# Head stages, residual loads and one more seven-product pair in an encoder layer on one core

## The chip, the cores and the metric

The kernel runs on one core of one Trainium2 chip. The metric is the device time of one execution in microseconds (us). Three executions of the kernel before the change took 1923.64, 1925.68 and 1930.04 us; the median is 1925.68.

The core's engines each work through their own list of instructions in order: TensorE (PE: products and transposes; PEld is its loading of weights), VectorE (DVE), ScalarE (ACT), GpSimd (POOL) and SyncE (SP, which here only issues DMA transfers). They wait for each other through semaphores. An instruction that waits holds up everything behind it on its engine or queue.

## The reference

One encoder layer over 256 tokens with 4096 features, float32.

```python
h = rms_norm(x, g_mix)
proj = h @ w_in            # c_q | c_kv | k_rope | gate_a | q_b | k_b | v_b | gate_b
# A: latent attention, 16 heads of 128 (+64 rotary)
q_a = rms_norm(c_q, g_q_latent) @ w_uq
kv = rms_norm(c_kv, g_kv_latent) @ w_ukv
y_a = rms_norm(mla_attention(q_a, kv, k_rope), g_out_mla) * silu(gate_a)
# B: dilated attention, 16 heads of 128, three (window, dilation) patterns
y_b = rms_norm(dilated_mixture_attention(q_b, k_b, v_b), g_out_dil) * silu(gate_b)
x = x + concat(y_a, y_b) @ w_out
ple = p @ w_ple
gate = sigmoid(rms_norm(x, g_ple) @ w_ple_gate)
out = rms_norm(x + ple * gate, g_final)
```

## The kernel before

**Products.** Every float32 operand is split into a high and a low half (ScalarE writes the high half, VectorE subtracts it from the source and writes the low half, `split`). A product of a 128-row piece is three matmuls: high by high, high by low, low by high (`mm`). Weights come from memory in tiles of 128 x 1024 (512 KB, the tile `raw`, four buffers, `RAW` at line 1738) through SyncE's queue, are split, and are used at once for two token tiles and two column halves: four products, twelve matmuls 512 wide.

**Seven-product pairs.** Two such row tiles can be taken together as a two-by-two block product with seven products in place of eight (Strassen's scheme in Winograd's form). `fast_steps` (line 1167) makes the four steps of a pair: more sums on VectorE, one product less on TensorE. The sums of the activations are made ahead (`x_sums`, `y_sums`). `FAST_QKV` (line 1552) says how many pairs each of the six blocks of q, k and v takes out of its 32 row tiles, in the order q, k, v of the first half and then of the second; `LEAD_QKV` how many plain steps come first; `spread` (line 1502) mixes plain steps and the steps of the pairs.

**The planner.** The order of instructions on all engines is written by the program itself while it builds. The main loop runs the product steps one after another. Between products it calls `advance` (line 417), which resumes side tasks: generators such as a head's attention. `Clock` (line 67) keeps an estimated time for each engine and each tile. A task has a due time, `due[task]`; it is resumed when that is at most `SOON` = 0.3 us past the estimated time of TensorE, `clock.free["pe"]`. `resume` (line 404) sets the due time from what the task has issued and, if the task yields a number, from that number.

**A head** (`attend`, line 573) has three stages that begin on TensorE. Dilated heads first transpose q and k. Then come the scores, into PSUM bank `s` (reserved by `take`, line 368); the softmax on VectorE and ScalarE; the transposes of the probabilities, into bank `t0` or `t1` (reserved by `turned`, line 378, which other tasks also use for their transposes: gates, normalised residuals, latents); a split; and the values, into bank `o`, reserved by `take`. The 16 dilated heads run beside the latent projection (some 509 to 682 us in the profile), the 16 latent heads beside their own up-projections and the first w_out products (some 1049 to 1224 us). The flag `"x dead"` (line 1621) is set between the two, after the gates' projections.

**After the latent heads**: `y_stats` and `gate_rest` normalise and gate the head outputs (transposes again), `split_y` splits them into `yT`, `y_sums` makes the sums for the pairs in tile T1. w_out is made as two half chunks (columns of residual blocks 6 and 7, the rows that need only the dilated heads), then three wide blocks of 1024 columns (`WIDE_O`) with 6, 6 and 4 pairs, then the other halves of blocks 6 and 7. The pairs of the first wide block use tile B4 for their differences, which held one of the gates.

**Residual x.** `load_res(c)` (line 1026) loads the 512 columns of x that residual block c adds, 512 KB, into tile T0 to T7. Before, all eight go through GpSimd's queue. Blocks 6 and 7 are asked for with the half chunks; blocks 2k and 2k + 1 at steps 8 and 9 after the start of wide block k (line 1657), once all latent heads are recorded. They are added when the block's pairs are done (`out_mid`).

All instructions that the planner records carry line 176 of its helper in the profile; groups are told apart by their tiles. Tile names there: `m`, `s`, `o`, `t` are PSUM banks, `raw` weights as loaded, `hi` and `lo` the halves, `Ah`, `Al`, `B`, `T`, `Q` the large tiles that are reused, weight halves among them.

Of the kernel before, what the change touches and what calls it, by code (L numbers as in the profile page):

```python
# [18 lines left out]
P = 128  # L19
# [3 lines left out]
HEADS = 16  # L23
# [186 lines left out]
def encoder_layer(ctx: ExitStack, tc: tile.TileContext, x, p, positions, g_mix, w_in, g_q_latent, w_uq,  # L210
                  g_kv_latent, w_ukv, g_out_mla, g_out_dil, w_out, w_ple, g_ple, w_ple_gate, g_final,
                  c_inv, c_dist, out):
    whole, clock = tc.nc, Clock()
    nc = Engines(whole, clock)
    x, p, out = x[0], p[0, 0], out[0]
# [10 lines left out]
    def slot(tag, shape, dtype=F32):  # L226
        names[tag] = names.get(tag, 0) + 1
        return clock.made(sp.tile([P, *shape], dtype, tag=tag, name=f"{tag}_{names[tag]}"), tag)
# [58 lines left out]
    G, at = {"mix": gT[:, :32]}, 0  # L287
# [11 lines left out]
    def turn_gains(i, at, n):  # L299
        tag = yield from turned()  # L300
        tp = bank(tag, [2 * S])
        nc.tensor.transpose(tp[:, :n], gains[:n, i], ident[:n, :n])
        yield
        nc.scalar.activation(gT[:, at:at + n], tp[:, :n], AF.Copy)
        give(tag)
# [51 lines left out]
    class Flags(set):  # L357
        at = {}
# [5 lines left out]
    flags, urgent, waiting, running = Flags(), [], [], []  # L364

    locks = set()

    def take(*tags):

        while any(t in locks for t in tags):  # L370
            yield
        locks.update(tags)
        yield max(clock.ready(t) for t in tags)

    def give(*tags):
        locks.difference_update(tags)
# [1 line left out]
    def turned():  # L378

        while True:  # L380
            open_ = [t for t in turns if t not in locks]
            if open_:
                tag = min(open_, key=clock.ready)
                locks.add(tag)
                yield clock.ready(tag)
                return tag
            yield

# [5 lines left out]
    begun, due = [-20.0], {}  # L394
# [3 lines left out]
    def spawn(task, later=False):  # L398
        urgent.append(task)
        due[task] = 0.0  # L400
        if later:
            lazy.add(task)

    def resume(pool, task):
        while True:
            clock.stage = 0.0
            got = next(task, "end")
            due[task] = max(clock.stage, due.get(task, 0.0), got if isinstance(got, float) else 0.0)
            if got == "end":
                pool.remove(task)  # L410
                due.pop(task, None)
                lazy.discard(task)
                return
            if not isinstance(got, float) or due[task] > clock.free["pe"] + SOON:
                return
# [76 lines left out]
    def done_a(i):  # L492
        def task(ps):
# [63 lines left out]
            pe = slot("T7", [2, S], F32R)  # L557
            T7["pe"] = pe
            tag = yield from turned()
            tp = bank(tag, [2, S])  # L560
            for t in range(NT):
# [11 lines left out]
    def attend(h, q_src, k_src, pe, v, y, dil):  # L573
# [19 lines left out]
        else:  # L593
            qT, kT = q_src, k_src
        at_s, at_o = "s", "o"
        yield from take(at_s)
        s = bank(at_s, [NT, S])
        for t in range(NT):
# [419 lines left out]
    x1 = {}  # L1018
# [5 lines left out]
        return tuple(q[:, kt % 4] for q in yT[kt // 4])  # L1024

    def load_res(c):
        before = {6: ("pe", 1), 7: ("scored", 0, HEADS - 1)}.get(c)
        while not (before in flags if before else all(("head", 0, h) in flags for h in range(HEADS))):
            yield
        x1[c] = slot(f"T{c}", [NT, 512])  # L1030
        nc.gpsimd.dma_start(x1[c], x[:, 512 * c:512 * (c + 1)].rearrange("(t p) k -> p t k", p=P))
        flags.add(("res", c))

    X1_TAGS = "Ah3", "Al3", ("B7a", "B7b"), "B4", "B6", "Al1", "B2", "B3"
# [220 lines left out]
    def out_mid(k, blk):  # L1255
        def task():
            ps, u = blk.ps, slot("Q0", [Q])
            x11, x21, x12, x22 = (x1[2 * k + h][:, t] for h in range(2) for t in range(NT))

            def add(d, a, b):  # L1260
                nc.vector.tensor_tensor(d, a, b, op=ALU.add)

            nc.scalar.activation(u, ps["M1"], AF.Copy)
            add(x11, x11, ps["M1"])
            add(u, u, ps["M6"])
            add(x12, x12, ps["M5"])
            add(x12, x12, u)
            yield
            add(u, u, ps["M7"])
            add(x22, x22, ps["M5"])  # L1270
            add(x21, x21, u)
            add(x22, x22, u)
            yield
        return task

    def out_done(k, blk):
        def task():
            quarters = ((0, 0, "M2"), (1, 1, "X"), (0, 1, "M3"), (1, 0, "M4"))
            for t, h, m in quarters:
                xc = x1[2 * k + h][:, t]  # L1280
                nc.vector.tensor_tensor(xc, xc, blk.ps[m], op=ALU.add)
            yield
            turns_ = [x1_turn(2 * k + h) for h in range(2)]
            for h in range(2):
                for t in range(NT):
                    c = 2 * k + h
                    nc.scalar.activation(junk, x1[c][:, t], AF.Square, accum_out=ss1[:, t, c:c + 1])
                yield from turns_[h]
        return task
# [198 lines left out]
    steps = []  # L1488
# [13 lines left out]
    def spread(n, lead, trail, extra=()):  # L1502

        rest = 32 - 2 * n - lead - trail
        order, debt, k = ["c"] * lead, 0.0, 0
        rate = (n * sum(FAST_COST) + rest * PLAIN_COST) / (n * sum(FAST_TIME) + rest * PLAIN_TIME)
        while k < 4 * n or rest:
            if k < 4 * n and (debt <= 0 or not rest):
                order.append("f")
                debt += FAST_COST[k % 4] - rate * FAST_TIME[k % 4]  # L1510
                k += 1
            else:
                order.append("c")
                rest -= 1
                debt += PLAIN_COST - rate * PLAIN_TIME
        order += ["c"] * trail
        for at in extra:
            order.insert(at, "e")
        return order

    def lay(blk, order, mid, done, ple=None):
        last = max(i for i, o in enumerate(order) if o == "f")
        n = order.count("f") // 4
        fast = (x for j in range(n) for x in blk.fast_steps(j))
        rest = list(range(2 * n, 16)) + list(range(16, 32))
        if blk.late:
            rest = rest[16 - 2 * n:] + rest[:16 - 2 * n]
        plain_ = (x for kt in rest for x in blk.plain_step(kt))
        for i, kind in enumerate(order):
            new = {"f": lambda: [next(fast)], "c": lambda: [next(plain_)], "e": lambda: ple}[kind]()  # L1530
            if i == last:
                new[-1].after = mid
            if i == len(order) - 1:
                new[-1].after = done
            for x in new:
                x.ring, x.ring_id = blk.ring, blk
            steps.extend(new)
        return len(steps) - len(order) + last

    def hook(at, f):  # L1540
        hooks.setdefault(at, []).append(f)

    def only(*tags):
        def go():
            turns[:] = tags
        return go
# [2 lines left out]
    G_BANKS = "m2", "m3", "s", "o", "m0", "m1", "t0", "t1"  # L1549
    H_BANKS = "m0", "m1", "t0", "t1", "m2", "m3", "s", "o"  # L1550
    Y_BANKS = "s", "o", "t0", "t1", "m0", "m1", "m2", "m3"
    FAST_QKV, LEAD_QKV = (3, 7, 7, 8, 8, 6), (18, 4, 4, 4, 4, 8)
    FAST_G, LEAD_G = (4, 7, 7, 7), (14, 6, 6, 4)
    FAST_O, LEAD_O = (6, 6, 4), (4, 5, 4)

# [24 lines left out]
    def allow(blk, tag, when):  # L1580
        allowed[tag, blk] = when
# [71 lines left out]
    for k in range(WIDE_O):  # L1653
        if k:
            hook(len(steps), only(*(("s", "o"), ("t0", "t1"))[k - 1]))
        for h in range(2):
            hook(len(steps) + 8 + h, lambda c=2 * k + h: spawn(load_res(c)))
        order = spread(FAST_O[k], LEAD_O[k], 4)
        blk = Block(w_out[:, 1024 * k:1024 * (k + 1)], lhs_y, y_s, "y_sums", order, lambda kt: [("yT", kt // 4)],
                    (G_BANKS, H_BANKS)[k % 2], "B4" if k < 2 else "Al1",  # L1660
                    WP + (["Ah3", "Al3", ("B7a", "B7b")], [("B7a", "B7b")], ["B3"])[k])
        blk.row = lambda kt: (kt + 16) % 32
        if k == 0:
            blk.fast_needs = [("gated", 0, c) for c in range(4)]
            blk.holds = blk.fast_needs
        else:
            blk.turn_needs = [("x1T", 2 * k - 2), ("x1T", 2 * k - 1)]
        lay(blk, order, out_mid(k, blk), out_done(k, blk))
        end = len(steps) - 1
        if k == 0:  # L1670
            for tag in ("Ah3", "Al3"):
                allow(blk, tag, lambda i, end=end: ("yT", 7) in flags and i < end)
            allow(blk, ("B7a", "B7b"), lambda i: ("gated", 0, 1) in flags)
        elif k == 1:
            allow(blk, ("B7a", "B7b"), lambda i, end=end: i < end)
# [119 lines left out]
    steps = [Old(i, *x) if isinstance(x, tuple) else x for i, x in enumerate(steps)]  # L1795
# [152 lines left out]
```

## Time and profile before

| what | us |
| --- | --- |
| median of three executions | 1925.68 |
| lowest, highest | 1923.64, 1930.04 |
| the profiled execution, its own time | 1922.69 |
| span of its instructions | 1920.9 |
| TensorE busy | 1897.0 |
| VectorE busy | 1635.0 |
| ScalarE busy | 1115.9 |

The profile is of one execution. A span of a matmul reaches beyond the start of the next one, since matmuls are pipelined: the time from start to start is what a matmul costs TensorE, and a short pause may not show as idle time at all. PEld, the loading of weights, shows such pauses better. A row of the waits names who waited for whom, the total in us, how often, and the longest. A row of the time line gives start, duration, what ran, and in square brackets the idle time before it and what ended it. A row of the chain of waits gives start and duration of one piece of the chain that ended last. A row of the stretches gives, for each engine, the busy time in it, then the granted TensorE clock, the busy share of the 16 DMA engines and GB/s.

### The profile page before, as it was taken

The numbers are of one execution on the slowest core, as the hardware profiler recorded it, in microseconds if no ns is written. First come the engines' busy times: TensorE is split into PE (matmuls) and PEld (weight loads), VectorE is DVE, ScalarE is ACT, GpSimd is POOL, SyncE is SP. The second block draws the span as 40 slices with busy tenths as digits, with TensorE's granted clock in tenths as the row PEclk, the third lists the DMA queues.
The fourth block names the chain that finished last, engine by engine and source line by source line (L and its number), as shares of the span: only waits on it lengthen the run. The fifth ranks groups of instructions, "written<-read, shape, count | busy, mean of one in ns | idle before, by whom it ended". The sixth has DMA issues, their size and how long they took to land.

```text
span 1920.9 us, 25936 instructions
## 1 busy us (share of the span) xinstructions
PE 1897.0 (99%) x9454; PEld 1615.9 (84%) x9454; DVE 1635.0 (85%) x2270; ACT 1115.9 (58%) x1518; POOL 40.8 (2%) x56
## 2 busy tenths in 40 slices
PE   9999999999999999999999999999999999999997
PEld 7888888888899988888888998878888887888887
DVE  6999989898877789899998678888887989889865
ACT  7655656564577755556556555656555555656543
POOL 1000000000000100000000001100000000000000
PEclk9999999999999999999999999999999999999999
DMA  8566766666654566666667444576666556566665
GB/s 274 185 204 215 219 207 201 198 206 197 181 154 136 148 194 192 194 207 195 213 203 199 131 121 143 160 257 202 196 195 199 182 195 215 190 220 204 214 196 176
DMA packets 159024, 370.61 MB, mean 193 GB/s; under 512 B 28548, under 2 KB 70640, under 8 KB 158640
## 3 DMA queue, kind: packets, MB, share of 16 engines
q1 hardware_dynamic: 157008, 361.82, 60.6%
q0 software_dynamic: 1888, 7.14, 1.1%
q8 instruction: 74, 1.21, 0.3%
q14 instruction: 54, 0.44, 0.1%
HBM read 364.72 MB, written 4.19 MB: 192 GB/s over the span
## 4 chain that ended last, share of the span: by engine, by line
PE 90%; DVE 5%; DMA 2%; ACT 1%; issue 1%; SPq 0%; DVEq 0%; ACTq 0%
PE m L176 51%; PE t L176 17%; PE s L176 11%; PE o L176 11%; DVE lo L176 1%; DVE T L176 1%; DMA raw<-in_w_out_dram 1%; DVE B L176 1%; DVE Al L176 1%; ACT hi L176 1%; ACT T L176 0%; DVE st L176 0%; DMA raw<-in_w_in_dram 0%; DMA raw<-in_w_ple_gate_dram 0%; DVE Ah L176 0%
## 5 line engine op out<-in xcount | busy, mean ns | idle before, releaser
L176 ACT ACTIVATE hi<-raw 128x1024 fp32r<-128x1024 f32 (+3 forms) x453 | 438.1, 976 | 344.5 <-PE t L176 90.0
L176 DVE TENSOR_TENSOR lo<-raw,hi 128x1024 fp32r<-128x1024 f32 (+3 forms) x453 | 502.3, 1118 | 112.5 <-ACT hi L176 109.4
L176 PE MATMUL m<-hi,Ah 128*128 128x512 f32 (+2 forms) x840 | 310.0, 381 | 3.5 <-DVE B L176 2.1
L176 PE MATMUL m<-hi,Al 128*128 128x512 f32 (+3 forms) x832 | 298.6, 372 | 0.0
L176 PE MATMUL m<-lo,Ah 128*128 128x512 f32 (+3 forms) x722 | 269.3, 373 | 0.8 <-DVE lo L176 0.8
L176 PE MATMUL m<-hi,B 128*128 128x512 f32 (+1 forms) x654 | 206.1, 365 | 1.0 <-DVE B L176 1.0
L176 DVE TENSOR_TENSOR B<-raw,B 128x1024 fp32r<-128x1024 f32 (+2 forms) x200 | 184.5, 932 | 16.3 <-ACT B L176 14.7
L176 PEld LDWEIGHTS m<-hi,Ah 128*128 128x128 f32 x840 | 157.9, 188 | 27.2 <-DVE B L176 2.8
L176 PEld LDWEIGHTS m<-hi,Al 128*128 128x128 f32 x832 | 155.9, 188 | 22.4
L176 ACT ACTIVATE B<-raw 128x1024 fp32r<-128x1024 f32 (+1 forms) x126 | 117.6, 941 | 85.1 <-DMA raw<-in_w_in_dram 24.4
L176 PEld LDWEIGHTS m<-lo,Ah 128*128 128x128 f32 x722 | 135.8, 188 | 20.9 <-DVE lo L176 3.1
L176 PEld LDWEIGHTS m<-hi,B 128*128 128x128 f32 x654 | 120.0, 189 | 19.6 <-issue 1.4
L176 PE MATMUL m<-lo,B 128*128 128x512 f32 (+1 forms) x327 | 118.9, 364 | 0.2 <-DVE lo L176 0.2
L176 PE MATMUL m<-B,Ah 128*128 128x512 f32 (+1 forms) x389 | 100.7, 360 | 0.0
L176 DVE TENSOR_TENSOR T<-raw,T 128x512 f32<-128x512 f32 (+2 forms) x101 | 77.8, 778 | 3.1 <-ACT T L176 1.7
L176 PE MATMUL t<-hi,Ah 128*128 128x512 f32 (+1 forms) x209 | 77.4, 386 | 0.0
L176 PEld LDWEIGHTS m<-B,Ah 128*128 128x128 f32 x389 | 66.6, 189 | 11.1 <-DVE B7b L176 0.2
L176 PE MATMUL m<-B,Al 128*128 128x512 f32 (+1 forms) x286 | 75.8, 345 | 0.0
L176 PEld LDWEIGHTS m<-lo,B 128*128 128x128 f32 x327 | 61.8, 189 | 10.2 <-DVE lo L176 1.6
L176 ACT ACTIVATE hi<-B 128x1024 fp32r<-128x1024 f32 x51 | 53.7, 1057 | 22.3 <-issue 8.6
L176 PE MATMUL t<-lo,Ah 128*128 128x512 f32 (+1 forms) x171 | 66.1, 387 | 0.0
L176 DVE TENSOR_TENSOR T<-t,T 128x512 fp32r<-128x512 f32 (+2 forms) x57 | 38.8, 684 | 30.2 <-ACT T L176 30.1
(501 smaller groups left out, 4025.7 us busy)
## 6 DMA issues: line engine op xcount, KB each, us to landing
raw<-in_w_in_dram SPq DMA_DIRECT2D x320, 512.0 KB, 4.3
raw<-in_w_out_dram SPq DMA_DIRECT2D x128, 512.0 KB, 4.5
raw<-in_w_ple_gate_dram SPq DMA_DIRECT2D x128, 512.0 KB, 4.6
raw<-in_w_in_dram SPq DMA_DIRECT2D x48, 384.0 KB, 3.3
raw_q<-in_w_uq_dram SPq DMA_DIRECT2D x32, 256.0 KB, 4.0
raw_k<-in_w_ukv_dram SPq DMA_DIRECT2D x16, 512.0 KB, 4.2
raw<-in_w_in_dram SPq DMA_DIRECT2D x16, 448.0 KB, 3.5
raw_r<-in_w_uq_dram SPq DMA_DIRECT2D x16, 256.0 KB, 3.7
```

Of the source, the lines that this page charges most:

```text
L176: return do(out, *rest, **named)
```

## The change

Three edits:

- A stage that begins on TensorE is handed out later. `take` for bank `s` or `o`, and `turned`, now yield a `Late` number, and `resume` adds 0.3 us to the due time for it, 0.45 us once `"x dead"` is set. This holds for every user of `turned`, heads or not.
- Residual blocks 0 to 5 are loaded through SyncE's queue, the one of the weights; 6 and 7 stay on GpSimd's. Within a wide block the two loads are asked for at steps 6 and 14 in place of 8 and 9, and block 1 waits for the last y sum.
- The third block of q, k and v (v of the first half) takes eight pairs in place of seven.

```diff
+    class Late(float):
+        pass
+
     def take(*tags):
 
         while any(t in locks for t in tags):
             yield
         locks.update(tags)
-        yield max(clock.ready(t) for t in tags)
+        at = max(clock.ready(t) for t in tags)
+        yield Late(at) if tags[0] in ("s", "o") else at
...
                 tag = min(open_, key=clock.ready)
                 locks.add(tag)
-                yield clock.ready(tag)
+                yield Late(clock.ready(tag))
                 return tag
...
             due[task] = max(clock.stage, due.get(task, 0.0), got if isinstance(got, float) else 0.0)
+            if isinstance(got, Late):
+                due[task] += 0.45 if "x dead" in flags else 0.3
...
     def load_res(c):
-        before = {6: ("pe", 1), 7: ("scored", 0, HEADS - 1)}.get(c)
+        before = {1: ("y_sums", 5), 6: ("pe", 1), 7: ("scored", 0, HEADS - 1)}.get(c)
         while not (before in flags if before else all(("head", 0, h) in flags for h in range(HEADS))):
             yield
         x1[c] = slot(f"T{c}", [NT, 512])
-        nc.gpsimd.dma_start(x1[c], x[:, 512 * c:512 * (c + 1)].rearrange("(t p) k -> p t k", p=P))
+        queue = nc.gpsimd if c > 5 else nc.sync
+        queue.dma_start(x1[c], x[:, 512 * c:512 * (c + 1)].rearrange("(t p) k -> p t k", p=P))
...
-    FAST_QKV, LEAD_QKV = (3, 7, 7, 8, 8, 6), (18, 4, 4, 4, 4, 8)
+    FAST_QKV, LEAD_QKV = (3, 7, 8, 8, 8, 6), (18, 4, 4, 4, 4, 8)
...
-            hook(len(steps) + 8 + h, lambda c=2 * k + h: spawn(load_res(c)))
+            hook(len(steps) + 6 + 8 * h, lambda c=2 * k + h: spawn(load_res(c)))
```

## The prediction

> **What bounds the kernel now.** I read the page first, then the busy time by stretches, then the waits of the weight loads, then the time line and the chain of waits where TensorE stood still.
>
> ```profile
> span 1920.9 us, 25936 instructions
> ...
> PE 1897.0 (99%) x9454; PEld 1615.9 (84%) x9454; DVE 1635.0 (85%) x2270; ACT 1115.9 (58%) x1518; POOL 40.8 (2%) x56
> ...
> PEclk9999999999999999999999999999999999999999
> ...
> PE 90%; DVE 5%; DMA 2%; ACT 1%; issue 1%; SPq 0%; DVEq 0%; ACTq 0%
> ```
>
> TensorE is busy 1897.0 of 1920.9 us, at its full clock in every slice, and it is 90% of the chain. So there are two ways to gain: fewer products, or fewer of the pauses in the remaining 23.9 us and in the smaller ones that overlapped spans hide. The stretches say where pauses are:
>
> ```profile
> core 0: us, PE busy (x) PEld busy (x) DVE busy (x) ACT busy (x) POOL busy (x), PEclk, DMA share, GB/s
> 97.00:180.00 83.00, 82.96 (x366) 68.21 (x365) 80.87 (x108) 46.49 (x55) 0.00 (x0) 1.00 0.66 210
> 180.00:262.00 82.00, 82.00 (x363) 67.72 (x363) 75.36 (x86) 48.05 (x53) 0.00 (x0) 1.00 0.71 223
> 262.00:344.00 82.00, 82.00 (x363) 67.91 (x362) 77.10 (x91) 47.63 (x51) 0.00 (x0) 1.00 0.64 201
> ...
> 509.00:682.00 173.00, 173.00 (x1078) 168.34 (x1077) 128.74 (x249) 117.86 (x235) 12.71 (x15) 1.00 0.52 146
> 1049.00:1224.00 175.00, 171.63 (x1234) 159.41 (x1233) 131.10 (x231) 97.48 (x194) 17.32 (x18) 1.00 0.46 137
> 1224.00:1255.00 31.00, 30.81 (x152) 25.26 (x151) 27.95 (x45) 20.77 (x29) 0.00 (x0) 1.00 0.55 174
> 1255.00:1265.00 10.00, 10.00 (x46) 8.26 (x45) 7.89 (x10) 3.48 (x4) 3.61 (x5) 1.00 0.93 328
> 1265.00:1275.00 10.00, 8.29 (x36) 6.32 (x35) 7.94 (x9) 5.48 (x6) 0.00 (x0) 1.00 0.88 308
> ```
>
> The projection blocks (97 to 344 us) have no pause worth the name. The latent heads (1049 to 1224) lose 3.4 us, and 1.7 us go in the ten us from 1265, right after ten us in which the DMA engines moved 328 GB/s at a share of 0.93. These are the two places that the change touches.
>
> **One more seven-product pair** (block 2, the first half of v: 7 becomes 8 of 16). The two built programs differ on TensorE by exactly three 128x512 products, 6606 to 6603; VectorE gets one 128x1024 and five 128x512 instructions more, ScalarE one of each.
>
> ```profile
> 1277.86 2.04 PE m L176 x9
> ...
> 1137.32 3.60 PE m L176 x30
> ...
> 1193.89 0.44 PE t L176 x4
> ```
> ```profile
> L176 DVE TENSOR_TENSOR lo<-raw,hi 128x1024 fp32r<-128x1024 f32 x13 | 15.9, 1219 | 1.1 <-ACT hi L176 1.1
> L176 DVE TENSOR_TENSOR T<-raw,T 128x512 f32<-128x512 f32 x16 | 11.0, 688 | 0.3
> ```
>
> A 512-wide product takes 2.04 / 9 = 0.227 us of TensorE (a 256-wide one 3.60 / 30 = 0.12, a transpose 0.11), so three are worth 0.68 us. VectorE pays 1.22 + 5 x 0.69 = 4.7 us: 75.4 + 4.7 = 80.1 in some 81.3 us of the stretch 180 to 262. That is hidden, by the row 97 to 180: there VectorE was busy 80.87 of 83 and TensorE still 82.96; and the stretch 262 to 344 is a block that has eight pairs already. Without the cover it would cost up to 4.7 - 0.7 = 4.0. I take -0.7.
>
> **The residual loads.** Before, all eight residual blocks are loaded through GpSimd's queue. GpSimd waits for nothing that the weights' queue waits for, so it runs ahead of the point where the code asks for a load:
>
> ```profile
> 1218.66 1.45 POOL L176 DMA_DIRECT2D T<-in_x_dram  x2
> 1255.46 3.61 POOL L176 DMA_DIRECT2D T<-in_x_dram  x5 [35.35 <-DVE B L176]
> ```
> ```profile
> 1257.65 8.14 DMA raw<-in_w_out_dram
> ...
> 1265.90 1.06 ACT Al L176
> ...
> 1266.99 1.24 DVE Al L176
> ```
> ```profile
> 1265.22 0.84 PE L176 MATMUL m<-Ah,Ah 128*128 128x512 f32 x3
> 1267.01 0.49 PE L176 MATMUL m<-Al,Ah 128*128 128x512 f32 x1 [0.95 <-ACT Al L176]
> 1268.27 1.43 PE L176 MATMUL m<-Al,Ah 128*128 128x512 f32 x5 [0.76 <-DVE Al L176]
> ```
> ```profile
> raw<-in_w_out_dram SPq DMA_DIRECT2D x128, 512.0 KB, 4.5
> ```
>
> At 1255.5 five loads of 512 KB leave at once, held up until then by one tile (T1) that the y sums still used. The weight load issued at 1257.65 then needs 8.14 us where 4.5 is the median; ScalarE and VectorE convert it late, and TensorE pauses: the third of three products starts at 1265.67 (1265.22 + 2 x 0.227), the next at 1267.01, the next at 1268.27, so 1.11 + 1.03 = 2.1 us beyond the pitch.
>
> The change sends blocks 0 to 5 down the weights' queue. In the built order 16, 16, 5, 28 and 6 weight loads stand between them, so the burst is gone: one load at 328 GB/s takes 524,288 / 328,000 = 1.6 us. That is covered by the converted halves ahead of TensorE and the four raw buffers: the burst asked for 5 x 1.6 = 8.0 us of DMA time in one go and TensorE felt 2.1 of them, so about 6 us are absorbed. The new wait on the weights' queue (block 1 waits for T1, released by the last y sum) holds the next weight loads; in VectorE's order the y sum's last instruction stands three rows behind the one those loads would wait for anyway, about 2 us (1.22 + 0.69), within the same 6. I take -2.1; bounds: 0 to -2.1 for the burst, and +1.6 for each load that is not covered.
>
> [...]
>
> **The margin.** A head's stage that begins on TensorE (transposes, scores, values) is now handed out when the planner's TensorE time is 0.3 us later than before (0.45 after "x dead"). Before, a stage could be placed up to 0.3 us ahead of its operands, and TensorE, which runs in order, stood in front of it. The waits of the weight loads in 1049 to 1224:
>
> ```profile
> PEld m L176 <- DVE B L176: 1.6, 1, 1.6
> PEld o L176 <- DVE T L176: 1.5, 4, 0.7
> PEld s L176 <- ACT T L176: 1.4, 4, 0.3
> PEld m L176 <- ACT Ah L176: 0.9, 1, 0.9
> PEld t L176 <- issue: 0.5, 2, 0.2
> PEld m L176 <- DVE lo L176: 0.4, 1, 0.4
> PEld t L176 <- ACT Al L176: 0.4, 1, 0.4
> PEld t L176 <- PE m L176: 0.2, 1, 0.2
> ```
>
> The banks of heads are o, s and t: 1.5 + 1.4 + 0.5 + 0.4 + 0.2 = 4.0 us, each pause at most 0.7, the size of the margin. The m rows (2.9 us) are weights converted late, which the margin does not address. How such a wait stands to lost time, at the largest:
>
> ```profile
> 1215.63 0.28 PE L176 MATMUL o<-T,B 128*128 128x256 f32 x1
> 1216.27 0.86 PE L176 MATMUL o<-T,B 128*128 128x256 f32 x5 [0.36 <-DVE T L176]
> ```
>
> Start to start 0.64 against a pitch of 0.12: 0.52 lost for a wait of 0.7. The view drops the smallest waits, which pull the other way. Bounds: 0 (the pause only moves) to -4.0; as nearly every pause is shorter than the margin I take -3.6. The dilated heads add nothing that I count: TensorE shows no idle time between 509 and 682.
>
> What is queued behind a later stage: all of its head's chain. Counted through both built orders with the pitches above, the last head's value product begins after 1197.4 us of TensorE work before and 1202.8 now; the last gate transposes at 1219.0 and 1227.1; the first seven-product pair of w_out, which reuses the gate's buffer B4, at 1232.3 and 1231.7. So 13.3 us of cover at this join shrink to 4.5. VectorE has five short instructions there, 5 x 0.69 = 3.5 us: still covered. I take 0.
>
> **Sum.** -0.7 - 2.1 - 3.6 = -6.4. The profiled execution took 1922.69 (span 1920.9 and 1.8 around it), 3.0 under the median of 1925.68; so 1916.3 for such an execution, and 1919.3 for the median.
>
> **The rivals.**
> *The pause only changes place.* In-order work is late either way, and behind each stage there is a converted weight that is not earlier for it. For it: 2.9 us of the waits above are late weights, and VectorE is at 131 of 175 us there. Against it: each head's pause is shorter than the margin. -0.7 - 2.1 = -2.8: 1922.9.
>
> *The join breaks* (slower). Place: the first pair of w_out, from the point where the chain from the last head through normalisation and gate to buffer B4 needs more than 4.5 us behind the last gate transposes. If it used all 13.3 us before, the 13.3 - 4.5 = 8.8 us become a pause, and the heads' gain is gone with it: -0.7 - 2.1 + 8.8 = +6.0, 1931.7. For it: VectorE is busy 27.95 of 31 us from 1224 to 1255, and two of the six y sums now fall behind the first pair instead of one. Against it: TensorE was busy 30.81 of those 31.
>
> *The queue does not do what it says.* Each of the six loads delays the weight behind it by its 1.6 us: 6 x 1.6 = 9.6, so -0.7 - 2.1 - 3.6 + 9.6 = +3.2, 1928.9. For it: the DMA share is already 0.66 and more beside the loads. Against it: the 6 us absorbed above.
>
> **How the numbers follow.** Forecast 0.55, moved pause 0.25, join 0.15, queue 0.05. What a measurement of this kernel can tell from no change is about 0.3%, 5.8 us. The forecast lies just beyond, with its own range from -4.5 to -9.9 (all 4.0 of the heads, and the 2.9 us of late weights too, with -0.7 and -2.1, is -9.7): I count 0.52 of its 0.55 as faster. Within 0.3%: 0.25 + 0.05 + 0.03 = 0.33. Slower: 0.15, the join. Range: from 1912.5 (-9.7 and the 3 us by which the profiled run already undercut the median) to 1929, which takes in the queue and leaves out the join.
>
> **What would show it.** Right: three 512-wide products fewer; GpSimd issuing only two residual loads around 1190 to 1220; no DMA share near 0.9 from 1250 to 1275 and no pause of an Al product there; the weight loads' waits for o, s and t in the heads' stretch under 1 us instead of 4.0. Wrong: those waits unchanged, or as much more on the m rows; TensorE idle between the last gate transposes and the first pair of w_out, with VectorE full (the join); a weight load of w_out of over 6 us behind a residual load, with TensorE waiting (the queue); or VectorE above 81 us with a pause between 180 and 262.

## The result, and the profile after

The changed kernel took 1916.41 us (median of five, 1915.94 to 1917.36), the kernel before 1927.4 beside it (1923.64 to 1930.04). The ratio is 0.9947, with a 95% interval of 0.9932 to 0.9961: 0.53% faster. In a later repeat it was 0.9951 (0.9938 to 0.9963), 1915.16 against 1924.56. The forecast was 1919.3 with a range of 1912.5 to 1929. The profiled execution went from 1922.69 to 1916.41, 6.3 us less, where the sum had 6.4; the one profiled in the repeat took 1918.24, 4.5 us less, so that the near match is partly luck.

The page of the changed kernel, its engines and the chain of waits:

```profile
PE 1892.6 (99%) x9451; PEld 1614.7 (84%) x9451; DVE 1636.3 (85%) x2276; ACT 1115.9 (58%) x1520; POOL 35.4 (2%) x50
...
PE 82%; DVE 11%; DMA 3%; issue 2%; ACT 2%; SPq 0%; ACTq 0%; DVEq 0%
```

Three products fewer (9454 to 9451). The chain runs through VectorE for 11% now, not 5%; that is the path by which the chain is followed back, and says nothing of lost time, since TensorE is as full as before. The stretches that the prediction looked at, in the same columns, in the changed kernel:

```profile
180.00:262.00 82.00, 81.93 (x362) 67.54 (x361) 79.47 (x93) 49.23 (x56) 0.00 (x0) 1.00 0.69 219
...
509.00:682.00 173.00, 173.00 (x1079) 168.58 (x1078) 129.40 (x249) 118.35 (x235) 12.69 (x15) 1.00 0.49 146
1049.00:1224.00 175.00, 173.51 (x1252) 162.61 (x1251) 128.63 (x227) 97.93 (x194) 15.56 (x17) 1.00 0.47 139
1224.00:1255.00 31.00, 31.00 (x152) 25.42 (x152) 29.36 (x48) 20.52 (x29) 0.00 (x0) 1.00 0.55 174
1255.00:1265.00 10.00, 10.00 (x45) 8.26 (x44) 9.93 (x12) 6.52 (x8) 0.00 (x0) 1.00 0.81 274
1265.00:1275.00 10.00, 10.00 (x46) 8.27 (x45) 9.93 (x12) 6.01 (x7) 0.00 (x0) 1.00 0.72 236
```

TensorE's idle time in the latent heads fell from 3.4 to 1.5 us, the 1.7 us after 1265 are gone, and GpSimd issues nothing there. The DMA share from 1255 to 1265 is still 0.81, not far from the 0.9 that the prediction had named as a sign, but no pause comes of it. The waits of the weight loads between 1049 and 1224 in the changed kernel:

```profile
PEld m L176 <- DVE lo L176: 1.4, 4, 0.7
PEld m L176 <- ACT Ah L176: 0.9, 1, 0.9
PEld o L176 <- DVE T L176: 0.6, 2, 0.4
PEld s L176 <- ACT T L176: 0.5, 2, 0.3
PEld t L176 <- issue: 0.3, 1, 0.3
```

The banks of the heads (o, s, t) wait 1.4 us in place of 4.0, where the prediction had asked for under 1, and the late weights (m) 2.3 in place of 2.9: the pauses did not move there. How far TensorE is ahead can be read from the products that it has started, here from the beginning of the span, first before, then changed:

```profile
0.00:1049.00 1049.00, 1045.01 (x4996) 888.12 (x4997) 922.47 (x1286) 633.68 (x844) 18.08 (x30) 1.00 0.65 197
0.00:1300.00 1300.00, 1290.74 (x6566) 1108.08 (x6567) 1119.28 (x1604) 775.88 (x1092) 39.01 (x53) 1.00 0.62 190
...
0.00:1900.00 1900.00, 1888.30 (x9384) 1607.42 (x9385) 1625.66 (x2238) 1112.71 (x1513) 40.84 (x56) 1.00 0.62 193
```
```profile
0.00:1049.00 1049.00, 1044.59 (x4999) 888.37 (x5000) 927.25 (x1292) 634.46 (x846) 18.05 (x30) 1.00 0.63 197
0.00:1300.00 1300.00, 1294.10 (x6599) 1113.65 (x6600) 1129.72 (x1620) 780.25 (x1099) 33.62 (x47) 1.00 0.61 190
...
0.00:1900.00 1900.00, 1890.22 (x9433) 1612.60 (x9434) 1630.62 (x2255) 1114.10 (x1517) 35.44 (x50) 1.00 0.61 194
```

At 1300 us it is 33 products further on a list that has lost three: 36 x 0.227 = 8.2 us. At 1049 it was 6 x 0.227 = 1.4. So 6.8 us come from the latent heads and the first w_out products, where the prediction had 3.6 + 2.1 = 5.7. The profile of the repeat has the same 6.8 (30 products), and the 1.4 up to 1049 shrink to 0.2 in it, so a difference of a few products says nothing. At 1900, where the products are 256 wide, the lead is 52 x 0.12 = 6.2 us: some 2 us are given back. Most of that is one pause that the profile of before does not have, by the time line of TensorE, the chain of waits and the time line of GpSimd in the changed kernel:

```profile
1784.41 0.61 PE L176 MATMUL m<-hi,B 128*128 128x512 f32 x2
1786.38 0.50 PE L176 MATMUL m<-lo,B 128*128 128x512 f32 x1 [1.36 <-DVE lo L176]
```
```profile
1773.64 8.90 DMA raw<-in_w_ple_gate_dram
```
```profile
1773.53 0.54 POOL L176 DMA_DIRECT2D B<-in_g_final_dram  x1 [14.39 <-PE t L176]
```

GpSimd issues a load of 1 MB (the final gain) at 1773.53; the weight load issued at 1773.64 takes 8.90 us, and TensorE waits: the second of two products started at 1784.64, the next at 1786.38, 1.5 us beyond the pitch. It looks like the pattern of the residual loads once more, with one large load. The change did not bring it: the kernel before issues the same load (at 1781.47 in its profile) with no pause (TensorE is busy 30.00 of the 30 us from 1770 there), and of the thirteen profiled executions that load the final gain in this way (both kernels and the runs e1 to e11 below) nine have a pause here, of 0.3 to 1.5 us, the pair alone (e3) among them.

### The profile page after: what moved, and what is told of

The parts are those of the page before. It is cut to its first block, busy times and chain, and to the rows that moved or that the text cites. A ratio compares the mean times of both kernels' runs of the same rounds, so it can differ in the third digit from the quotient of the medians.

```text
span 1914.6 us, 25920 instructions
## 1 busy us (share of the span) xinstructions
PE 1892.6 (99%) x9451; PEld 1614.7 (84%) x9451; DVE 1636.3 (85%) x2276; ACT 1115.9 (58%) x1520; POOL 35.4 (2%) x50
## 4 chain that ended last, share of the span: by engine, by line
PE 82%; DVE 11%; DMA 3%; issue 2%; ACT 2%; SPq 0%; ACTq 0%; DVEq 0%
PE m L176 48%; PE t L176 15%; PE s L176 10%; PE o L176 9%; DVE lo L176 3%; DVE B L176 3%; DVE T L176 2%; DMA raw<-in_w_ple_gate_dram 2%; DVE Ah L176 1%; DMA raw<-in_w_in_dram 1%; DVE Al L176 1%; ACT hi L176 1%; DVE st L176 0%; ACT T L176 0%; ACT B L176 0%
## 5 line engine op out<-in xcount | busy, mean ns | idle before, releaser
L176 PE MATMUL m<-hi,Ah 128*128 128x512 f32 (+3 forms) x836 | 308.5, 381 | 2.3 <-ACT hi L176 1.8
L176 PE MATMUL m<-B,Ah 128*128 128x512 f32 (+1 forms) x421 | 110.3, 363 | 0.1
L176 DVE TENSOR_TENSOR T<-raw,T 128x512 f32<-128x512 f32 (+2 forms) x107 | 85.2, 808 | 5.0 <-ACT T L176 3.4
L176 PE MATMUL m<-B,Al 128*128 128x512 f32 (+1 forms) x302 | 82.9, 348 | 0.0
L176 PEld LDWEIGHTS m<-B,Ah 128*128 128x128 f32 x421 | 72.3, 189 | 12.4 <-DVE B7b L176 0.5
L176 PE MATMUL t<-hi,Ah 128*128 128x512 f32 (+1 forms) x220 | 81.4, 386 | 0.0
L176 PE MATMUL t<-hi,Al 128*128 128x512 f32 x170 | 65.2, 389 | 0.0
```

What stands on the lines that cost most here:

```text
L176: return do(out, *rest, **named)
```

## The experiments

The theory: each part acts where it stands, the margin on the heads' pauses, the residual loads on the burst, and the gains add up. The rivals: the planner merely drew another order; or a load hurts by being on a queue of its own.

| label | kernel | median, us | ratio to before, 95% interval |
| --- | --- | --- | --- |
| e1_margin | before + margin | 1919.90 | 0.9968 (0.9956 to 0.9981) |
| e2_residual | before + residual loads | 1920.77 | 0.9981 (0.9972 to 0.9989) |
| e3_pair | before + pair | 1923.95 | 0.9998 (0.9989 to 1.0007) |
| e4_paced_gpsimd | before + paced loads on GpSimd | 1921.35 | 0.9984 (0.9975 to 0.9993) |
| e5_no_margin | changed, no margin | 1921.96 | 0.9991 (0.9983 to 1.0000) |
| e6_no_residual | changed, old residual loads | 1917.37 | 0.9966 (0.9953 to 0.9978) |
| e7_no_pair | changed, seven pairs | 1916.38 | 0.9964 (0.9950 to 0.9978) |
| e8_latent_only | changed, margin in the latent part alone | 1917.60 | 0.9970 (0.9958 to 0.9981) |
| e9_changed_again | changed | 1915.16 | 0.9951 (0.9938 to 0.9963) |
| e10_margin_less | changed, margin 0.2 | 1918.86 | 0.9965 (0.9953 to 0.9978) |
| e11_margin_double | changed, margin 0.9 | 1921.09 | 0.9982 (0.9973 to 0.9990) |
| e12_final_gain_in_turn | changed, final gain in the weights' queue | 1913.86 | 0.9946 (0.9932 to 0.9959) |

The kernel before had medians of 1924.1 beside e1 to e4, 1924.1 beside e5 to e8 and 1924.6 beside e9 to e12.

### The margin alone

The `Late` class, the two `yield`s and the addition in `resume`, on the kernel before.

> The kernel before with the margin alone. Each part acts where it stands: the waits of the weight loads for o, s and t between 1049 and 1224 fall from 4.0 us to about 1.4 as in the full change, the burst at 1255 and its pause of 2.1 us stay, and the time falls by 4 to 5 us, 0.2 to 0.27%. Rival, a chance order: the margin merely draws another order of all engines, the waits of the heads fall but late weights take their place, and the time is within 0.1% of before.

0.32% faster (0.19 to 0.44%), 4.2 us by the medians. The heads' waits fell exactly as in the full change, to 0.6 + 0.5 + 0.3 us. The burst did not stay at 1255, though that had been expected: the y sums end later, so tile T1 is free later, and GpSimd let the five loads go at 1298. Its time line, the stretch, the chain of waits, TensorE's pause and the four us after it in this run:

```profile
1297.79 3.60 POOL L176 DMA_DIRECT2D T<-in_x_dram  x5 [76.69 <-DVE B L176]
```
```profile
1300.00:1310.00 10.00, 10.00 (x46) 8.28 (x45) 7.91 (x8) 4.56 (x5) 1.39 (x2) 1.00 0.97 367
```
```profile
1303.34 9.45 DMA raw<-in_w_out_dram
```
```profile
1325.39 0.33 PE L176 MATMUL s<-ident,T 128*128 128x128 f32 x1 [1.97 <-DVE T L176]
```
```profile
1326.00:1330.00 4.00, 4.00 (x13) 3.34 (x14) 3.34 (x5) 2.40 (x5) 0.00 (x0) 0.61 0.63 203
```

A DMA share of 0.97, a weight load of 9.45 us, and a pause of 2.0 us, to which the chain of waits leads from that load. After the pause the clock was granted at 0.61 of full for four us. From 1300 to 1500 this run starts 882 products and the changed kernel 902: 20 x 0.227 = 4.5 us, so the burst costs more here than the 2.1 us at 1255, and part of what the margin gives is lost again. Chance order falls in its strong form: the gain is there, though the whole order after the heads differs. What is by chance is where the burst lands.

### The residual loads alone, and paced on GpSimd

```diff
         x1[c] = slot(f"T{c}", [NT, 512])
+        if c < 6:
+            nc.vector.tensor_scalar(pace[:, :2], ident[:, :2], 1.0, None, op0=ALU.mult)
+            nc.gpsimd.tensor_tensor(pace[:, 2:], pace[:, :2], pace[:, :2], op=ALU.add)
         nc.gpsimd.dma_start(x1[c], x[:, 512 * c:512 * (c + 1)].rearrange("(t p) k -> p t k", p=P))
```

The first kernel has the change's `load_res` and its steps; the second has its steps and its wait for the y sum too, but stays on GpSimd's queue with the lines above.

> The kernel before with the residual loads in the weights' queue alone (with their new steps and the wait for the last y sum). Burst: the pause of 2.1 us after 1265 goes, the heads' waits stay at 4.0 us, the time falls by 2 to 3 us (0.1 to 0.16%). If the burst is also what makes the runs of the kernel before differ by 6.4 us (1923.64 to 1930.04), the fall of the median is larger, 4 to 6 us, and five runs agree within 2 us as those of the changed kernel do (1915.94 to 1917.36). Rival, only the heads count: under 1 us.

> The kernel before with the residual loads still in GpSimd's queue, but held back: ahead of each of the six loads VectorE writes two columns at the point where the load is asked for, and GpSimd reads them (six small instructions on each). Burst: no five loads at once, no weight load of 8 us at 1257, the time as with the weights' queue (within 1 us of that run). Rival, the queue itself: a load beside the weights on a queue of its own still slows them, and most of the pause stays; 2 us or more above the run with the weights' queue.

0.19% and 0.16% faster, 3.4 and 2.8 us by the medians, where 2 to 3 had been expected. The heads' waits stay at 4.0 and 4.1 us. The ten us from 1255 and from 1265 in the kernel with the weights' queue, then in the one paced on GpSimd:

```profile
1255.00:1265.00 10.00, 10.00 (x46) 8.27 (x45) 8.45 (x11) 4.63 (x6) 0.00 (x0) 1.00 0.78 259
1265.00:1275.00 10.00, 10.00 (x45) 8.15 (x44) 9.55 (x11) 6.35 (x8) 0.00 (x0) 1.00 0.75 253
```
```profile
1255.00:1265.00 10.00, 10.00 (x45) 8.27 (x45) 9.17 (x13) 5.70 (x7) 1.30 (x2) 1.00 0.73 229
1265.00:1275.00 10.00, 10.00 (x46) 8.27 (x45) 9.49 (x11) 6.03 (x8) 0.00 (x0) 1.00 0.72 251
```

No pause in either: TensorE is busy 10.00 of 10 us in all four rows, where the kernel before had 8.29 after 1265. GpSimd's six paced loads leave 13 to 70 us apart (1262.63, 1276.00, 1345.15 and so on). The queue is not what matters here; that the loads leave one at a time is. One expectation missed: the burst is not what makes the runs of the kernel before differ. Without it eleven runs still spread from 1918.66 to 1923.90.

### The pair alone

`FAST_QKV` as in the change, on the kernel before.

> The kernel before with the eighth seven-product pair of the third block alone. Three products of 0.227 us: 0.7 us less, 0.04%. Rival, VectorE as the bound in that block (79.5 of 82 us busy in the changed kernel): 0 or up to 2 us more. Either is small against the spread of the kernel before; the number of products and the pauses between 180 and 262 us decide.

0.9998, with 0.9989 to 1.0007: no change that can be told, as 0.04% could not be. Its profile has the three products fewer (9451), and TensorE is idle 0.5 us between 180 and 262 (81.47 of 82); the changed kernel with seven pairs is idle 0.25 there, so neither the gain of 0.7 us nor VectorE as the bound is shown.

### The changed kernel less one part

> The changed kernel without the margin. If the parts add up, it keeps the residual loads' and the pair's gain and loses the margin's: 4 to 5 us over the changed kernel, 0.1 to 0.2% under before, with the heads' waits for o, s and t back near 4 us. Chance order: no relation to the run of the margin alone.

> The changed kernel with all residual loads in GpSimd's queue and at the old steps. The margin alone left a burst of loads somewhere in w_out: here too, with a pause of 2 to 4 us, and 2.5 to 5 us over the changed kernel. Rival, the burst falls where enough is converted: within 1 us of the changed kernel.

> The changed kernel with seven pairs in the third block: 0.7 us over the changed kernel by the three products; with VectorE as the bound there (79.5 of 82 us busy), 0 or less.

Without the margin 0.09% are left of the gain, so taking it out of the whole costs 0.4%, a little more than it gave alone; the waits are back at 4.6 us, as the rows of this run between 1049 and 1224 say:

```profile
PEld s L176 <- ACT T L176: 1.9, 4, 0.6
...
PEld o L176 <- DVE T L176: 1.6, 5, 0.7
...
PEld t L176 <- issue: 0.5, 2, 0.3
...
PEld t L176 <- ACT Al L176: 0.4, 1, 0.4
PEld t L176 <- PE m L176: 0.2, 1, 0.2
```

With the old residual loads the burst is at 1296.75, and TensorE waits 1.05 and 0.27 us for a VectorE result at 1323; from 1300 to 1500 it starts 892 products, against 902 in the changed kernel, 2.3 us. The median is 1.0 us above the changed kernel's first median and 2.2 above the repeat, less than the 2.5 expected, and the intervals overlap. Without the pair the ratio is 0.9964, but its interval and that of the repeat (0.9951) overlap; by its median of 1916.38 nothing was lost. Neither tells 0.7 us.

> The changed kernel with the margin in the latent part alone (0.45 after x dead, 0 before in place of 0.3). The prediction counted nothing for the dilated heads: within 1 us of the changed kernel. Rival, the dilated heads and the gates' transposes ahead of x dead gain as well: 2 us or more over it.

Inconclusive: 1917.6 is 1.2 us above the changed kernel's first median and 2.4 above the repeat, over the 1 us of the first expectation and on either side of the 2 us of the rival, with intervals that overlap. In the profile TensorE has no idle time from 509 to 682 in either kernel.

### The size of the margin

```diff
-                due[task] += 0.45 if "x dead" in flags else 0.3
+                due[task] += 0.2 if "x dead" in flags else 0.3
```

and the same with 0.9.

> The changed kernel again, beside before on the same chip, as the measure for the three kernels that follow and for the single parts: 1916.5 us, 0.35 to 0.5% under before. Parts that add up: the margin alone took 4.2 us off, the residual loads alone 3.4, the pair alone 0.2, together 7.8.

> The changed kernel with a margin of 0.2 in place of 0.45 us in the latent part. If the margin works by its size, the waits of the weight loads for o, s and t between 1049 and 1224 lie between the 1.4 us of 0.45 and the 4.0 us without, about 2.5, and the time 1 to 3 us over the changed kernel. Chance order: no order by size; the waits or the time fall outside these two.

> The changed kernel with a margin of 0.9 us in the latent part. By size: the waits for o, s and t fall under 1 us, but the last gate transposes come 4.1 us of TensorE work later again (1231.2 by count of the built order), and the first seven-product pair of w_out stands close behind them: a pause at the join, so the same time or up to 4 us over the changed kernel. Rival: fewer waits and no join, 1 us less.

With 0.2 the heads' waits are 3.0 us, here from 1049 to 1224, then the same view with 0.9, whole:

```profile
PEld m L176 <- DVE B L176: 2.8, 1, 2.8
PEld s L176 <- ACT T L176: 2.1, 6, 0.8
PEld m L176 <- ACT Ah L176: 0.9, 1, 0.9
PEld o L176 <- DVE T L176: 0.5, 1, 0.5
PEld t L176 <- issue: 0.4, 2, 0.2
```
```profile
PEld m L176 <- DVE B L176: 3.2, 1, 3.2
PEld m L176 <- ACT Ah L176: 0.9, 1, 0.9
```

So the waits of o, s and t go 4.6, 3.0, 1.4 and none for margins of 0, 0.2, 0.45 and 0.9: by size, as the theory has it. The waits of the late weights (m) do not: 2.9, 3.7, 2.3 and 4.1. One product near 1180 makes most of that difference. It waits for a result of VectorE (`B`) in the runs with 0, 0.2 and 0.9, 1.4, 2.6 and 3.0 us by TensorE's time line, and not at all with 0.45; so the size of the margin does not decide that wait, and the order that the planner happens to draw may.

The time goes 1922.0, 1918.9, 1915.2 and 1921.1. With 0.2 it is 3.7 us over the repeat of the changed kernel, a little more than the 1 to 3 expected, and the late weights have a part in that. With 0.9 there are two causes, that late weight and the join. TensorE, VectorE and two stretches of the run with 0.9:

```profile
1176.70 0.80 PE L176 MATMUL m<-hi,Ah 128*128 128x512 f32 x1 [3.02 <-DVE B L176]
...
1249.44 0.60 PE L176 MATMUL t<-ident,B 128*128 128x128 f32 x4
1249.80 0.48 PE L176 MATMUL m<-hi,Ah 128*128 128x512 f32 x1
1252.81 0.50 PE L176 MATMUL m<-lo,Ah 128*128 128x512 f32 x1 [2.54 <-DVE lo L176]
...
1255.00 0.63 PE L176 MATMUL m<-B7b,Ah 128*128 128x512 f32 x1
1255.42 0.63 PE L176 MATMUL m<-B7a,Ah 128*128 128x512 f32 x1
```
```profile
1250.08 0.88 DVE L176 SCALAR_TENSOR_TENSOR Al<-Al,gT,t 128x256 f32<-128x256 f32 x2 [1.07 <-PE t L176]
1250.87 0.68 DVE L176 TENSOR_TENSOR B<-raw 128x512 f32<-128x512 f32 x1
1251.47 0.69 DVE L176 TENSOR_TENSOR B<-raw,raw 128x512 f32<-128x512 f32 x1
1252.07 0.69 DVE L176 TENSOR_TENSOR lo<-raw,hi 128x512 fp32r<-128x512 f32 x1
```
```profile
1176.50:1180.00 3.50, 3.30 (x12) 3.01 (x13) 3.43 (x6) 0.56 (x2) 0.00 (x0) 0.50 0.57 182
...
1253.00:1258.00 5.00, 4.83 (x14) 3.49 (x14) 4.96 (x6) 1.06 (x1) 0.00 (x0) 0.66 0.70 211
```

In the heads, the late weight makes TensorE idle for 3.02 us, and the clock was granted at 0.50 of full behind it. At the join, the last gate transposes stand right in front of the first pair, VectorE makes five short instructions, as many as the prediction had counted there, in 2.7 us (1250.08 to 1252.76), and TensorE starts the low-half product 2.8 us late. After that pause the clock was granted at 0.66 of full over five us, and products came every 0.43 us (1255.00, 1255.42) in place of 0.227. The two places cost about the same. Counted from 1049, the run has started 17 products fewer than the changed kernel by 1249 (1361 and 1378), 3.9 us, and 36 fewer by 1262 (1398 and 1434), 8.2 us. Some 2 us of that are won back later: the median is 5.9 us over the repeat. The expectation of up to 4 us had left out the late weight and the clock.

### The final gain in turn

```diff
-    hook(wide_end + 2, lambda: (load_g(0), load_g(1), spawn(late_gains(), True)))
+    for n in range(4):
+        hook(wide_end + 2 + 2 * n, lambda n=n: load_g(n // 2, n % 2))
+    hook(wide_end + 9, lambda: spawn(late_gains(), True))
```

`load_g(i, h)` loads half of a tile, 512 KB, through SyncE's queue.

> The changed kernel with the two loads of the final gain (1 MB each, GpSimd's queue) cut into four of 512 KB and put into the weights' queue two steps apart, as the residual loads were. If such a burst is behind the pause of 1.5 us at 1784 (a weight load of 8.9 us) in the changed kernel's profile, the pause goes and the time is 1 to 1.5 us less. Rival, that load was slow by chance: no difference beyond 0.5 us.

The stretch from 1740 to 1800 in the changed kernel, and in this one:

```profile
1740.00:1800.00 60.00, 58.64 (x259) 48.23 (x258) 54.53 (x61) 34.75 (x37) 1.10 (x2) 1.00 0.69 235
```
```profile
1740.00:1800.00 60.00, 60.00 (x266) 49.72 (x265) 54.46 (x61) 36.60 (x39) 0.00 (x0) 1.00 0.68 217
```

The pause is gone, and the median is 1.3 us under that of the repeat, as expected; but the two ratios (0.9946 and 0.9951) cannot be told apart, and four of the thirteen profiled executions that load the gain through GpSimd have no pause either. That the load costs this time is likely, not shown. It is the lowest median measured.

## Why the prediction was right, and where its sizes were off

**The pair.** Right: three products fewer, VectorE at 79.47 of 82 us where 80.1 had been worked out, and no pause to speak of (81.93 of 82). That the three products are worth 0.7 us of the whole is below what the runs can tell.

**The residual loads.** The mechanism was right, and the queue as a rival fell: spaced loads show no pause, on either queue (10.00 of 10 us busy from 1265 to 1275 on both). The size was low, if anything: 2.1 us taken, 0.19% alone, which is 3.7 us of 1924 (interval 2.1 to 5.4). The 2.1 us were read from one execution, and the price of a burst was not the same in every run: with the margin alone it fell elsewhere, with a weight load of 9.45 us and a clock granted at 0.61 behind the pause, and cost about 4.5 us; in the changed kernel with the old loads it cost 2.3.

**The margin.** The mechanism was right: the heads' waits fell with its size. The moved pause, as a rival, fell for the change as it was made, since the late weights wait no more than before; with margins of 0.2 and 0.9 they do wait more (3.7 and 4.1 us in place of 2.9), so it did not fall in general, and that 0.45 escapes it looks like luck of the order. The size was low: 3.6 us were taken. Alone, the margin gave 4.2 us by the medians, 6.2 by the ratio of 0.32% (3.7 to 8.5), with a burst in it that cost more than before. In the profile the heads and the first w_out products gave 6.8 us, of which the burst had 2.1, so 4.7 are left; against the changed kernel without the margin it is 22 products from 1049 to 1300 (1600 and 1578), 5.0 us. The step that was mis-sized is the bound of 4.0 us from the weight loads' waits. Of these 4.0 only 2.6 went, not 3.6: the prediction called the longest wait, 0.7, the size of the margin, which is 0.45. The late weights gave 0.6 more, which the prediction had put at nothing. The rest, some 1.5 of the 4.7, is in no row of the view. It drops the smallest waits, and their sum was not inside the bound; that they make up the difference is argued, not shown.

**The join.** No pause came at 4.5 us of cover, as taken. With 0.9, where 4.1 of the 4.5 were to be used up, it broke, at the place named: from the start of the last gate transposes to the product that waits took 3.4 us there (1249.44 to 1252.81), less than 4.5, as the prediction had it. No run has a cover between the two, so where exactly it breaks is not shown.

**The sum.** In the profile 6.3 us against 6.4, but errors cancel in it: the parts gave more, and a pause of 1.5 us at 1784 that the prediction did not look for took some back. Against the median of its neighbours the change gave 9.4 to 11.0 us, so the forecast of 1919.3 was 2.9 too high for the first runs. The profiled execution of before (1922.69) was faster than all five runs beside the changed kernel, and it has no pause at the final gain, where nine of the thirteen have one; that it held fewer pauses than a usual one, which makes a sum from it low for the median, fits this but is not shown. The lower end of the range does not follow from its own terms either: 1925.68 - 3.0 - 9.7 is 1913.0, not 1912.5. Parts alone give 0.32 + 0.19 + 0.02 = 0.53% by the ratios, the whole 0.53 and 0.49%; by the medians they give 4.2 + 3.4 + 0.2 = 7.8 us, the whole 9.4 to 11.0. With intervals of about 0.1% to either side, the runs do not contradict that the parts add up, and they cannot tell more. One part does act on another: the margin alone moves the burst to a dearer place.

## What to carry to other kernels

TensorE, 99% busy here, takes its work in order, and a planner that handed stages out a little early made it stand in front of them, 4.0 us by the weight loads' waits in the latent heads; a margin of 0.45 us, about the size of the usual pause, left 1.4 of them and paid. Twice that lost most of the gain again, 5.9 us by the median, half at the next join and half where a weight came late, so count the cover at the join, and read the waits of everything else on the engine, before making it larger. GpSimd's queue, which waited for nothing that the weights' queue waits for, ran ahead of the code here and let five loads go together at 1255.46, as soon as one tile came free, and a weight load beside them took 8.14 us where 4.5 is the median: look for several loads issued at one instant and a slow weight load beside them, and put such loads in turn with the stream that they disturb or hold them back. A profiled execution at the low end of the runs may give a sum that is too small for the median.

## What was not expected of the hardware

In two runs the granted TensorE clock was low behind pauses of two to three us. In the run with a margin of 0.9 an idle time of 2.54 us (to 1252.81) was followed, after 1.5 us in which products came as close as 0.23 us (1253.15, 1253.38), by some 2.5 us of products at 0.43 us each, and the granted clock was 0.66 from 1253 to 1258; behind its idle time of 3.02 us (to 1176.70) the products at 1177.30, 1177.72 and 1178.15 are 0.42 and 0.43 us apart, and the granted clock was 0.50 from 1176.5 to 1180. In the run with the margin alone the granted clock was 0.61 from 1326 to 1330, behind idle times of 1.97 and 0.27 us (to 1325.99). The changed kernel with the old residual loads has idle times of 1.05 and 0.27 us at the same place, and over its whole profiled execution a mean granted clock of 0.998, the same as the changed kernel's. The run with 0.2 had an idle time of 2.56 us (to 1178.30), and from the second product behind it on they came 0.23 us apart:

```profile
1178.30 0.50 PE L176 MATMUL m<-hi,Ah 128*128 128x512 f32 x1 [2.56 <-DVE B L176]
1178.64 0.40 PE L176 MATMUL m<-lo,Ah 128*128 128x512 f32 x1
1178.87 0.39 PE L176 MATMUL m<-hi,Ah 128*128 128x512 f32 x1
1179.10 0.88 PE L176 MATMUL o<-T,B 128*128 128x256 f32 x6
```

So products at 0.43 us followed idle times of 2.54 and 3.02 us, and products at 0.23 us one of 2.56. What decides between the two is not shown.
